# Selection credit that counts other VectorE work, a free step in each recurrence, and attention's second pair moved behind the first `w_pa` job

## The chip, the cores and the metric

The kernel runs on one core of one Trainium2 chip. The metric is the device time of one execution in microseconds, as the median of several runs. Before the change it is 1357.88 us (three runs, 1356.63 to 1357.95).

## The reference

One layer of a hybrid block, batch 1, 512 tokens, width 2048, all in float32:

```python
h = rmsnorm(x, norm_w)
proj = h @ w_in                       # a_q a_f a_i a_g | c_q c_kv k_idx w_idx | b_g | m_a m_b
y_a = hgrn2_branch(a_q, a_f, a_i, a_g, ...)      # gated recurrence, 8 heads of 128, chunks of 64
y_b = dsa_branch(c_q, c_kv, k_idx, w_idx, ...)   # indexer scores -> top 128 keys per query -> attention
merged = sigmoid(m_a) * (y_a @ w_pa) + sigmoid(m_b) * (y_b @ w_pb)
out = rmsnorm(x + merged @ w_out, final_norm_w)
```

Branch A computes, per head, `o = sum over earlier tokens` of decayed key-value products. Branch B scores all visible keys with 16 index heads, keeps the 128 best per query, and runs softmax attention over them with a relative-position bias. Each branch's result is multiplied by a SiLU gate.

## The kernel before, in words

Every large product is made in three float32r passes (`mm3`, L75 to L77): each operand is split into a high and a low part, and high*high, high*low and low*high are accumulated in PSUM. A weight tile is loaded by SyncE (L128), its high part is copied by ScalarE and its low part is subtracted by VectorE (`split`, L71 and L72, tiles `wh` and `wl`).

TensorE is fed by a list of jobs that runs once, in order: projections of x (`feat_job`, `ai_job`), gate products with a seven-product scheme (`pair_job`), the index heads, then the part this change touches, then the two branch projections `w_pa` and `w_pb` and the output product. A `feat_job` with two column tiles does 12 matmuls of 512 columns per weight tile and column tile, evacuates a finished tile, and calls `pump()` (twice as often in the `w_pa` jobs).

`pump()` is what mixes the small work in. There are lanes named hgrn, top, att, norm, misc and t5; each holds Python generators, and one call advances the first generator of each lane to its next `yield`, in that order of lanes. All instructions go to their engine's queue in the order in which they are emitted, and each engine works its queue off in that order. So nothing is decided at run time: where a step stands in the emission sets what it waits behind.

- **hgrn** runs the recurrence of head pairs 3, 2, 0, 1, one generator (`hgrn_gen(p)`) each. It makes levels 1 to 7: at each level TensorE computes small score matmuls (`hl`) from the tile `hqk`, VectorE multiplies `hqk` by the level's decay (L763, 1024 columns) and takes scores into a mask (L769). The scores of a level read the `hqk` that the level before has multiplied. After the levels come transposes of k (`hkt`), copied by ScalarE to `hkd`, state products (`hp`), the states `hst`, outputs (`ho`), a norm by a matmul with ones (`hz`), and the gated result `hy`, split in two and stored to the DRAM tile `ya_d` (L859).
- **top** is the selection (`top_gen`): 3 blocks of queries, 16 rounds each of MAX and MATCH_REPLACE on VectorE (L631, L632) over 256, 384 and 512 columns of the score mask `M`. It works on credit: each call adds 2.7 less `R.load`, each round costs 0.4 + 0.27 per block of 128 columns, and rounds are emitted while credit is positive. `R.load` is set by the hgrn lane to about what its step costs VectorE.
- **att** runs attention for a pair of heads (`att_gen(p)`), and starts once the selection is finished. Its steps: the mask with bias `MB` (GpSimd), scores `lA`, `lB`, `lC` with VectorE adds (L930), exponentials, transposes `tA` to `tC`, values `po`.

The queries, keys and values of head pair p are made by `uqkv(p)`: a job for the queries (`uq_evac`, tiles `aq`) and a job for keys and values (`ukv_job`, tiles `ak`, `av`). All projection results go through one PSUM pool `mmp` of four buffers; a product may start when VectorE and ScalarE have read the buffer's last content.

The order of the jobs from the index on: `ai_job(3)`, `ai_job(2)`, `af_aq(0)`, `af_aq(1)`, `open_att` (which runs all but the last pending recurrence to its end at once), `uqkv(0)`, the gate job of four column tiles (`gate_job(44)`, eight weight tiles; it loads `y_a` back from `ya_d` into the tiles `yh` and `yl`, and after its seventh weight tile `end_hgrn` finishes the last recurrence and loads heads 2 and 3), `uqkv(1)`, and eight `w_pa` jobs with `uqkv(2)` and `uqkv(3)` behind those with j = 4 and j = 8.

Of the kernel before, what the change touches and what calls it, by code (L numbers as in the profile page):

```python
# [43 lines left out]
STILL, MOVED, RANK = 16, 48, 16  # L44
# [6 lines left out]
def hybrid_block(ctx, tc, x, w_in, w_uq, w_qidx, w_ukv, w_pa, w_pb, w_out, rel_bias, final_norm_w,  # L51
# [4 lines left out]
    w_in, w_uq, w_qidx, w_ukv = w_in[0], w_uq[0], w_qidx[0], w_ukv[0]  # L56
# [13 lines left out]
    def split(hi, lo, src):  # L70
        A.activation(hi, src, AF.Copy)  # L71
        V.tensor_tensor(lo, src, hi.bitcast(F32), op=OP.subtract)  # L72
# [22 lines left out]
    yb_d = dram.tile([2, H, 128, T], F32, name="yb_d")  # L95
# [17 lines left out]
    def leave(name):  # L113
        pools.pop(name)[0].__exit__(None, None, None)

    R = SimpleNamespace(load=0.0)


    specs = []
# [16 lines left out]
    def weight_places(at):  # L136
        return [wpool.tile([128, WCAP + 64], FR, name=name)[:, at:at + WCAP] for name in ("wh", "wl")]

    def pair_sums(t, at):


        b = t.rearrange("p (q n) -> p q n", q=4)
        sv = R.g.tile([128, 4, 256], F32, name="sv", bufs=R.sv)
        vh, vl = (a.rearrange("p (q n) -> p q n", q=4) for a in weight_places(at))
        V.tensor_tensor(sv[:, 0:2, :], b[:, 1:3, :], b[:, 0:1, :].to_broadcast([128, 2, 256]), op=OP.add)  # L145
        V.tensor_tensor(sv[:, 2, :], sv[:, 1, :], b[:, 1, :], op=OP.add)
        V.tensor_tensor(sv[:, 3, :], sv[:, 2, :], b[:, 3, :], op=OP.add)
        bh = R.g.tile([128, 3, 256], FR, name="bh", bufs=3)
        bl = R.g.tile([128, 3, 256], FR, name="bl", bufs=3)
        A.activation(bh, b[:, 1:4, :], AF.Copy)  # L150
# [6 lines left out]
    def prep(i, ahead=3):  # L157
        while issued[1] < min(i + ahead, len(specs)):
            j = issued[1]
            if specs[j][3:4] == ("pair",) and not hasattr(R, "g"):  # L160
                if j > i + 1 and lanes["norm"]:
                    break
                open_pairs()
            load_ahead()
            _, kc, n = specs[j][:3]
            t = raws.pop(j)
            if specs[j][3:4] == ("pair",):
                halves[j] = pair_sums(t, 0 if specs[j][4] else R.at)
                issued[1] += 1
                continue  # L170
            if len(specs[j]) > 3 and isinstance(specs[j][3], str):
                both = R.s2.tile([128, 2, WCAP], FR, name="wk", tag=specs[j][3])
                hi, lo = both[:, 0, :], both[:, 1, :]
            else:
                hi, lo = weight_places(*specs[j][3:] or (0,))
            split(hi[:, :kc * n], lo[:, :kc * n], t[:, :kc * n])
            halves[j] = tuple(a[:, :kc * n].rearrange("p (k n) -> p k n", k=kc) for a in (hi, lo))
            issued[1] += 1

# [20 lines left out]
    def drain(name):  # L200
        lane = lanes[name]
        while lane:
            for _ in lane[0]:
                pass
            lane.popleft()

    jobs, hg = [], {}

    def feat_job(src, col, ntile, nk, kc, rhs, evac, before=None, width=T, after=None, place=0,
                 often=False):  # L210
        at = len(specs)
        n = ntile * 128
        for k in range(0, nk, kc):
            specs.append(([(0, n, src[k * 128:(k + kc) * 128, col:col + n])], kc, n, place))

        def run():
            if before:
                before()
            ps = [mmp.tile([128, T], F32, name="acc")[:, 0:width] for _ in range(ntile)]
            for i in range(nk // kc):  # L220
                prep(at + i)
                wh, wl = halves.pop(at + i)
                for c in range(ntile):
                    for k in range(kc):
                        kk = i * kc + k
                        rh, rl = rhs(kk)
                        s = slice(c * 128, c * 128 + 128)
                        mm3(ps[c], wh[:, k, s], wl[:, k, s], rh, rl, kk == 0, kk == nk - 1)
                        if often and k == 1:
                            pump()  # L230
                    if kk == nk - 1:
                        evac(c, ps[c])
                    if ntile < 4 or c % 2:
                        pump()
                if after and i in after:
                    after[i]()

        jobs.append(run)
# [377 lines left out]

    def top_gen():

        credit = 0.0
        V.memset(R.M[:, 0:128], 0.0)  # L620
        for b in range(4):
            V.memset(R.M[0:64, MO[b] + b * 128 + 64:MO[b] + b * 128 + 128], NEG)
        for b in (1, 2, 3):
            m = R.M[:, MO[b]:MO[b] + b * 128 + 128]
            for i in range(16):
                while credit <= 0:
                    yield
                    credit += 2.7 - R.load
                credit -= 0.4 + 0.27 * (b + 1)
                m8 = R.s.tile([128, 8], F32, name="m8", bufs=2)  # L630
                V.max(m8, m)  # L631
                V.match_replace(m, m8, m, GONE)  # L632
                if i == 15:
                    V.tensor_scalar(m, m, -2e38, NEG, op0=OP.is_gt, op1=OP.mult)
# [83 lines left out]
    def aq_evac(p):  # L718
        def evac(c, ps):
            if c == 0:  # L720
                hg[p, "q"] = place(p, [128, 2, T], F32, "hq", "hq")
            q = hg[p, "q"][:, c, :]
            A.activation(q, ps, AF.Sigmoid)
            V.scalar_tensor_tensor(q, ps, 128 ** -0.5, q, op0=OP.mult, op1=OP.mult)
            if c == 1:
                lanes["hgrn"].append(hgrn_gen(p))
        return evac

    def hgrn_gen(p):
# [11 lines left out]
        q, k = qk[:, 0], qk[:, 1]  # L741
        qf, kf = (a.rearrange("p c t -> p (c t)") for a in (q, k))
        yield
        for _ in range({2: 1, 0: 2, 1: 2}.get(p, 0)):
            yield

        def scores(l, ps):
# [24 lines left out]
        for l in range(1, 8):  # L772
            R.load = (0, 2.9, 2.2, 2.0, 1.9, 1.8, 1.5, 1.4)[l]
            if l == 4:
                G.memset(S, 0.0)
            if l == 1:
                first = bank("hl")
                scores(0, first)
            ps = bank("hl")
            scores(l, ps)  # L780
            tot = decay(l)
            if l == 1:
                take(0, first)
            if l < 6:
                take(l, ps)
            else:
                m = 1 << (l - 1)
                for h in range(0, 128, 2 * m):
                    A.activation(S[h:h + m, :, h + m:h + 2 * m],
                                 ps[h:h + m, 0:8 * m].rearrange("p (n t) -> p n t", n=8), AF.Copy)  # L790
            if l == 6:
                for h in range(0, 128, 32):
                    A.activation(S[h:h + 32, :, h:h + 32], near[h:h + 32], AF.Copy)
            yield

        R.load = 0.0
        kd = R.h.tile([128, 2, 3, 128], F32, name="hkd")
# [57 lines left out]
        for c in range(2):  # L855
            y = [place(p, [128, T], FR, f"hy{i}", (("hkd", "hst"), ("hq", "hS"))[i][c]) for i in range(2)]
            split(*y, sq[:, c])
            for i in range(2):
                late[1].append(lambda y=y[i], i=i, h=2 * p + c: SP.dma_start(ya_d[i, h], y.bitcast(F32)))  # L859
        yield  # L860


    at_ = {}

    def uq_evac(p):
        def evac(c, ps):
            if c == 0:
                at_[p, "q"] = [R.a.tile([128, 2, T], FR, name=f"aq{i}") for i in range(2)]
            hi, lo = (a[:, c, :] for a in at_[p, "q"])
            A.activation(hi, ps, AF.Copy, scale=128 ** -0.5)  # L870
            V.scalar_tensor_tensor(lo, ps, 128 ** -0.5, hi.bitcast(F32), op0=OP.mult, op1=OP.subtract)
        return evac
# [150 lines left out]
    def open_pairs():  # L1023
        drain("norm")
        drain("misc")
        flush()
        flush()
        leave("norms")
        R.g = enter("pairs")
        R.g.tile([128, STILL], F32, name="gap")  # L1030
        R.sv, R.at = 2, STILL
# [105 lines left out]
    c_rhs = lambda k: (R.cqh[:, k, :], R.cql[:, k, :])  # L1137
# [56 lines left out]
        feat_job(w_in, p * 256, 2, NK, 4, x_rhs, aq_evac(p))  # L1194

    def uqkv(p):
        feat_job(w_uq, p * 256, 2, 4, 4, c_rhs, uq_evac(p), place=RANK)
        ukv_job(p)

    jobs.append(end_index)  # L1200
# [10 lines left out]
    def load_y(y, src, h0, h1):  # L1211
        for h in range(h0, h1, 2):
            for i in range(2):
                SP.dma_start(y[i][h // 4][:, h % 4:h % 4 + 2, :].bitcast(F32),
                             src[i, h:h + 2].rearrange("h p t -> p h t"))
# [20 lines left out]

    def y_rhs(name):
        return lambda k: tuple(y[k // 4][:, k % 4, :] for y in getattr(R, name))

    uqkv(1)  # L1240
    jobs.append(lambda: load_y(R.yb, yb_d, 0, 2))

    mh, ml, mg = [], [], {}

# [76 lines left out]
    for j in range(0, NK, 2):  # L1321
        if j + 2 < NK:
            jobs.append(lambda j=j: load_gates(16, j + 2))
        feat_job(w_pa, j * 128, 2, H, 4, y_rhs("ya"), pa_evac(j), often=True)
        if j in (4, 8):
            uqkv(j // 4 + 1)
        if j in (6, 10):
            jobs.append(lambda h=j // 2 - 1: load_y(R.yb, yb_d, h, h + 2))
    jobs.append(open_merge)
# [230 lines left out]
```

## Time and profile before

| | |
|---|---|
| median of 3 runs | 1357.88 us |
| profiled execution, its own time | 1356.24 us |
| its span, first to last instruction | 1354.4 us |
| TensorE busy | 1339.9 us (99%) |
| VectorE busy | 1070.7 us (79%) |
| ScalarE busy | 656.1 us (48%) |
| GpSimd busy | 41.3 us (3%) |
| DMA | 205.82 MB, mean 152 GB/s |
| mean granted TensorE clock | 0.997 |

The time outside the span is 1356.24 - 1354.4 = 1.8 us. A busy TensorE is not TensorE at its peak: ends of matmuls are modelled, and a matmul that waits a little shows as a longer distance between two starts. In the timelines below a row is a start, a duration, and in brackets the idle time before it with what ended it. The stretch from 690 us (end of the index) to 960 us (start of the `w_pa` jobs) is where the recurrences, the selection and attention's first pair run.

### The profile page before, as it was taken

How to read it: one execution, taken by the hardware profiler on the slowest of the kernel's cores; microseconds unless marked ns; L12 is line 12 of the kernel's file. 1: busy time of each engine (PE TensorE's matmuls, PEld its weight loads, DVE VectorE, ACT ScalarE, POOL GpSimd, SP SyncE). 2: the span in 40 equal slices, each digit the busy share in tenths (PEclk: the TensorE clock that was granted, in tenths of full speed). 3: DMA queues.
4: the chain of work that ended last, by engine and by line, in shares of the span. 5: the costliest groups of instructions: out<-in, count | busy, mean ns of one | idle time of the engine just before them, and what ended most of it. 6: DMA issues, size and time to landing. Idle time of an engine off the chain costs nothing.

```text
span 1354.4 us, 26556 instructions
## 1 busy us (share of the span) xinstructions
PE 1339.9 (99%) x10884; PEld 1242.7 (92%) x10884; DVE 1070.7 (79%) x1705; ACT 656.1 (48%) x1039; POOL 41.3 (3%) x54
## 2 busy tenths in 40 slices
PE   9999999999999999999999999999999999999997
PEld 9988999999999999999999787788888888899996
DVE  7777889998898888886789889585556658899856
ACT  6455554455544444444764454635443433454434
POOL 3000000000000000000000000020101100000000
PEclk9999999999999999999999999999999999999999
DMA  6343445543445444445324523244855556643454
GB/s 240 94 124 109 141 143 157 160 146 111 127 141 156 140 141 140 141 143 169 126 77 127 171 78 127 81 161 145 291 176 197 180 186 210 210 157 115 158 208 173
DMA packets 141290, 205.82 MB, mean 152 GB/s; under 512 B 8672, under 2 KB 82032, under 8 KB 141040
## 3 DMA queue, kind: packets, MB, share of 16 engines
q1 hardware_dynamic: 140592, 203.78, 47.1%
q8 instruction: 85, 1.39, 0.4%
q10 hardware_dynamic: 576, 0.35, 0.1%
q14 instruction: 37, 0.30, 0.1%
HBM read 168.42 MB, written 35.68 MB: 151 GB/s over the span
## 4 chain that ended last, share of the span: by engine, by line
PE 90%; DVE 5%; ACT 2%; DMA 1%; issue 1%; SPq 0%; ACTq 0%
PE pp L75 15%; PE pp L77 15%; PE pp L76 15%; PE acc L75 12%; PE acc L77 12%; PE acc L76 12%; PE hl L80 1%; PE ho L80 1%; DMA wr<-in_w_in_dram 1%; DVE wl L72 1%; PE sc L75 1%; PE sc L76 1%; PE sc L77 1%; DVE hqk L763 1%; DVE M L632 1%
## 5 line engine op out<-in xcount | busy, mean ns | idle before, releaser
L150 ACT ACTIVATE bh<-wr 128x768 fp32r<-128x768 f32 x128 | 108.2, 845 | 216.9 <-issue 108.8
L152 ACT ACTIVATE wh<-sv 128x512 fp32r<-128x512 f32 x256 | 152.2, 623 | 85.3 <-DVE sv L145 68.1
L75 PE MATMUL pp<-sh,wh 128*128 128x256 f32 x624 | 172.8, 277 | 0.0
L77 PE MATMUL pp<-sh,wl 128*128 128x256 f32 x624 | 172.8, 277 | 0.0
L76 PE MATMUL pp<-sl,wh 128*128 128x256 f32 x624 | 172.7, 277 | 0.0
L72 DVE TENSOR_TENSOR wl<-wr,wh 128x1024 fp32r<-128x1024 f32 (+1 forms) x104 | 125.3, 1204 | 56.8 <-ACT wh L71 56.5
L154 DVE TENSOR_TENSOR wl<-sv,wh 128x1024 fp32r<-128x1024 f32 x128 | 156.4, 1222 | 6.1
L153 DVE TENSOR_TENSOR bl<-wr,bh 128x768 fp32r<-128x768 f32 x128 | 122.2, 955 | 48.4 <-ACT bh L150 47.8
L71 ACT ACTIVATE wh<-wr 128x1024 fp32r<-128x1024 f32 (+1 forms) x104 | 108.0, 1040 | 104.8 <-PE acc L76 54.5
L75 PE MATMUL acc<-xh,wh 128*128 128x512 f32 x304 | 121.7, 400 | 0.0
L77 PE MATMUL acc<-xh,wl 128*128 128x512 f32 x304 | 118.8, 391 | 0.0
L76 PE MATMUL acc<-xl,wh 128*128 128x512 f32 x304 | 118.5, 390 | 0.0
L75 PEld LDWEIGHTS pp<-sh,wh 128*128 128x128 f32 x624 | 117.3, 188 | 0.0
L76 PEld LDWEIGHTS pp<-sl,wh 128*128 128x128 f32 x624 | 117.3, 188 | 0.0
L77 PEld LDWEIGHTS pp<-sh,wl 128*128 128x128 f32 x624 | 117.3, 188 | 0.0
L75 PE MATMUL pp<-xh,bh 128*128 128x256 f32 x416 | 114.9, 276 | 0.0
L77 PE MATMUL pp<-xh,bl 128*128 128x256 f32 x416 | 114.9, 276 | 0.0
L76 PE MATMUL pp<-xl,bh 128*128 128x256 f32 x416 | 114.9, 276 | 0.0
L75 PE MATMUL acc<-yh,wh 128*128 128x512 f32 x256 | 100.2, 391 | 0.0
L77 PE MATMUL acc<-yh,wl 128*128 128x512 f32 x256 | 99.8, 390 | 0.0
L76 PE MATMUL acc<-yl,wh 128*128 128x512 f32 x256 | 99.7, 390 | 0.0
L145 DVE TENSOR_TENSOR sv<-wr 128x512 f32<-128x512 f32 x128 | 87.8, 686 | 8.2 <-DMA wr<-in_w_out_dram 4.1
(385 smaller groups left out, 3618.5 us busy)
## 6 DMA issues: line engine op xcount, KB each, us to landing
wr<-in_w_in_dram SPq DMA_DIRECT2D x136, 512.0 KB, 3.6
wr<-in_w_out_dram SPq DMA_DIRECT2D x32, 512.0 KB, 3.8
mg<-gate_d SPq DMA_DIRECT2D x48, 256.0 KB, 4.4
gate_d<-c SPq DMA_DIRECT2D x44, 256.0 KB, 5.0
wr<-in_w_in_dram SPq DMA_DIRECT2D x36, 256.0 KB, 2.9
wr<-in_w_pa_dram SPq DMA_DIRECT2D x16, 512.0 KB, 4.3
wr<-in_w_pb_dram SPq DMA_DIRECT2D x16, 512.0 KB, 4.2
wr<-in_w_qidx_dram SPq DMA_DIRECT2D x8, 512.0 KB, 3.4
```

The lines of the kernel that those rows point to most:

```text
L71: A.activation(hi, src, AF.Copy)
L72: V.tensor_tensor(lo, src, hi.bitcast(F32), op=OP.subtract)
L75: PE.matmul(ps, lh, rh, start=first, stop=False, skip_group_check=True)
L76: PE.matmul(ps, lh, rl, start=False, stop=False, skip_group_check=True)
L77: PE.matmul(ps, ll, rh, start=False, stop=last, skip_group_check=True)
L80: PE.matmul(ps, l, r, start=first, stop=last, skip_group_check=True)
L145: V.tensor_tensor(sv[:, 0:2, :], b[:, 1:3, :], b[:, 0:1, :].to_broadcast([128, 2, 256]), op=OP.add)
L150: A.activation(bh, b[:, 1:4, :], AF.Copy)
L152: A.activation(vh[:, i:i + 2, :], sv[:, i:i + 2, :], AF.Copy)
L153: V.tensor_tensor(bl, b[:, 1:4, :], bh.bitcast(F32), op=OP.subtract)
L154: V.tensor_tensor(vl, sv, vh.bitcast(F32), op=OP.subtract)
L632: V.match_replace(m, m8, m, GONE)
```

## The change

It has five pieces.

1. The selection's credit: each call adds 2.95 (was 2.7) less `R.load`, and less `R.extra`, which is 1.2 for each weight tile split (L72) and 0.7 for each recurrence query tile (L724) emitted since the last call.
2. In `hgrn_gen`, one call passes between level 1 and level 2 in which the generator does nothing and `R.load` is 0. The idle calls ahead of level 1 go from 2 to 1 for pairs 0 and 1, and stay 1 for pair 2 and 0 for pair 3.
3. `R.load` is set to 0 in those idle calls and at the end.
4. `uqkv(1)` moves from behind the gate job to behind the first `w_pa` job, and the load of branch B's heads 0 and 1 with it.
5. Before the query job of pair 1 the lanes top and att are drained.

```diff
-    R = SimpleNamespace(load=0.0)
+    R = SimpleNamespace(load=0.0, extra=0.0)
...
             split(hi[:, :kc * n], lo[:, :kc * n], t[:, :kc * n])
+            R.extra += 1.2
...
-        credit = 0.0
+        credit = R.extra = 0.0
...
                 while credit <= 0:
+                    R.extra = 0.0
                     yield
-                    credit += 2.7 - R.load
+                    credit += 2.95 - R.load - R.extra
...
             V.scalar_tensor_tensor(q, ps, 128 ** -0.5, q, op0=OP.mult, op1=OP.mult)
+            R.extra += 0.7
...
         yield
-        for _ in range({2: 1, 0: 2, 1: 2}.get(p, 0)):
+        R.load = 0.0
+        for _ in range({2: 1, 0: 1, 1: 1}.get(p, 0)):
             yield
...
             yield
+            if l == 1:
+                R.load = 0.0
+                yield
...
         yield
+        R.load = 0.0
...
-        feat_job(w_uq, p * 256, 2, 4, 4, c_rhs, uq_evac(p), place=RANK)
+        feat_job(w_uq, p * 256, 2, 4, 4, c_rhs, uq_evac(p), place=RANK,
+                 before=lambda: p == 1 and (drain("top"), drain("att")))
         ukv_job(p)
...
-    uqkv(1)
-    jobs.append(lambda: load_y(R.yb, yb_d, 0, 2))
...
         feat_job(w_pa, j * 128, 2, H, 4, y_rhs("ya"), pa_evac(j), often=True)
-        if j in (4, 8):
+        if j in (0, 4, 8):
             uqkv(j // 4 + 1)
+        if j == 0:
+            jobs.append(lambda: load_y(R.yb, yb_d, 0, 2))
```

Three places show how instructions move. Each row is the kernel's line, the operation, output and inputs, and the output's shape; the changed file's lines are up to eight higher (its L742 and L767 are L739 and L763 before, its L879 is L871, its L1223 is L1214).

**VectorE in `uqkv(0)`.** `aq` is the low part of a query tile, `ak` and `av` those of keys and values, `wl` of a weight tile; `hqk` and `hnear` belong to the recurrence of pair 1; MAX and MATCH_REPLACE with `m` and `M` are selection rounds. Before:

```order
L871 SCALAR_TENSOR_TENSOR aq_10563<-acc,aq_10562 128x512
L739 TENSOR_TENSOR hqk<-hq,hf 128x1024
L871 SCALAR_TENSOR_TENSOR aq_10563<-acc,aq_10562 128x512
L72 TENSOR_TENSOR wl<-wr,wh 128x1024
L72 TENSOR_TENSOR ak_10595<-acc,ak_10594 128x512 x2
L72 TENSOR_TENSOR av_10597<-acc,av_10596 128x512 x2
L763 TENSOR_TENSOR hqk<-hqk,hf 128x2x512
L765 TENSOR_TENSOR tot_10715<-hf 128x512
L769 COPY_PREDICATED hnear<-levels,hl 128x256 x2
L72 TENSOR_TENSOR wl<-wr,wh 128x1024
L763 TENSOR_TENSOR hqk<-hqk,tot_10715 128x2x256x2
```

In the change, up to the first level's decay:

```order
L879 SCALAR_TENSOR_TENSOR aq_10547<-acc,aq_10546 128x512
L742 TENSOR_TENSOR hqk<-hq,hf 128x1024
L633 MAX m_10560<-M 128x8
L634 MATCH_REPLACE M<-m_10560,M 128x512
L879 SCALAR_TENSOR_TENSOR aq_10547<-acc,aq_10546 128x512
L633 MAX m_10577<-M 128x8
L634 MATCH_REPLACE M<-m_10577,M 128x512
L633 MAX m_10580<-M 128x8
L634 MATCH_REPLACE M<-m_10580,M 128x512
L72 TENSOR_TENSOR wl<-wr,wh 128x1024
L72 TENSOR_TENSOR ak_10588<-acc,ak_10587 128x512 x2
L767 TENSOR_TENSOR hqk<-hqk,hf 128x2x512
```

and behind it, up to the second level's decay:

```order
L769 TENSOR_TENSOR tot_10678<-hf 128x512
L773 COPY_PREDICATED hnear<-levels,hl 128x256 x2
L72 TENSOR_TENSOR av_10590<-acc,av_10589 128x512 x2
L633 MAX m_10712<-M 128x8
L634 MATCH_REPLACE M<-m_10712,M 128x512
L72 TENSOR_TENSOR wl<-wr,wh 128x1024
L767 TENSOR_TENSOR hqk<-hqk,tot_10678 128x2x256x2
```

Four selection rounds of 512 columns, which stood before `open_att`, now stand inside this job, three of them ahead of `ak`; and the first level's decay stands ahead of `av`, since its scores now come before the value products on TensorE.

**TensorE in `open_att`.** The recurrence of pair 0 runs to its end here, with no projection matmuls between its stages. Before, the state products `hp` have projection matmuls on both sides, and the last of these are followed by `ho` and `hz`:

```order
L80 MATMUL hp<-hv,hkd 128x128 [waits Activation_49]
L80 MATMUL hp<-hv,hkd 128x128 x2
L75 MATMUL acc<-xh_91,wh 128x512
L76 MATMUL acc<-xl_94,wh 128x512
L77 MATMUL acc<-xh_91,wl 128x512
```

In the change the same stage has none:

```order
L808 MATMUL hkt<-ident,hqk 128x128 [waits PE_49]
L808 MATMUL hkt<-ident,hqk 128x128 x2
L80 MATMUL hp<-hv,hkd 128x128 [waits Activation_49]
L80 MATMUL hp<-hv,hkd 128x128 x2
L80 MATMUL ho<-hS,hv 128x128 [waits PE_49,Pool_49]
L80 MATMUL ho<-hS,hv 128x128
L80 MATMUL ho<-hqk,hst 128x128 [waits Activation_49]
```

The transposes and the state products have moved into the stretch without cover.

**TensorE at the end of the gate job.** Before, the query job of pair 1 follows (here behind the last value matmul `po` of head 1):

```order
L77 MATMUL po<-PT,av_10597 128x128
L75 MATMUL acc<-cqh,wh 128x512 [waits Activation_49]
L76 MATMUL acc<-cql,wh 128x512
L77 MATMUL acc<-cqh,wl 128x512
L75 MATMUL acc<-cqh,wh 128x512
```

In the change the first `w_pa` job follows; `DMAHW` names the semaphore of a load:

```order
L77 MATMUL acc<-xh_91,wl 128x512
L75 MATMUL acc<-yh,wh 128x512 [waits DMAHW7_49,Activation_49]
L76 MATMUL acc<-yl,wh 128x512 [waits DMAHW0_49]
L77 MATMUL acc<-yh,wl 128x512 [waits DVE_49]
L75 MATMUL acc<-yh,wh 128x512
L76 MATMUL acc<-yl,wh 128x512
L77 MATMUL acc<-yh,wl 128x512
L75 MATMUL acc<-yh,wh 128x512 [waits DMAHW2_49]
L76 MATMUL acc<-yl,wh 128x512 [waits DMAHW3_49]
L77 MATMUL acc<-yh,wl 128x512
```

The seventh matmul of that job is the first to read head 2 of `y_a`, and waits for the load of heads 2 and 3, which is issued at the end of the gate job's seventh weight tile; the 60 matmuls of `uqkv(1)` no longer stand between.

## The prediction

> **What bounds the kernel.** I read the page's head, then the waits of TensorE, then stretches of the timeline around the places where the change moves work.
>
> ```profile
> span 1354.4 us, 26556 instructions
> PE 1339.9 (99%) x10884; PEld 1242.7 (92%) x10884; DVE 1070.7 (79%) x1705; ACT 656.1 (48%) x1039; POOL 41.3 (3%) x54
> ```
>
> TensorE is the bound, and the change adds or removes no work on it. So only its waits can move. The table of waits for the whole run holds, in the stretch that is touched:
>
> ```profile
> PE hl L80 <- DVE hqk L763: 1.6, 3, 0.7
> PE hl L80 <- issue: 0.9, 1, 0.9
> PE hz L80 <- ACT hzh L71: 0.7, 2, 0.4
> PE hz L80 <- DVE hzl L72: 0.5, 2, 0.3
> ```
>
> ```profile
> 715.39 0.70 PE L80 MATMUL hl<-hqk 128*32 128x32 f32 x32 [0.70 <-DVE hqk L763]
> 766.04 0.45 PE L80 MATMUL hl<-hqk 128*32 128x32 f32 x31 [0.57 <-DVE hqk L763]
> 832.89 0.52 PE L80 MATMUL hl<-hqk 128*32 128x32 f32 x36 [0.35 <-DVE hqk L763]
> ```
>
> Three waits for a decay on VectorE (1.6 us), one of 0.9 us in which nothing shows what was awaited, and four for the norm in `open_att`. That is all a better order could win: 3.7 us. The `open_att` waits have a tail, seen in the windows (columns: busy time of PE, PEld, DVE, ACT, POOL, then granted clock, DMA share, GB/s):
>
> ```profile
> 866.00:868.00 2.00, 1.27 (x3) 0.56 (x3) 0.93 (x2) 1.95 (x5) 0.00 (x0) 1.00 0.00 0
> 868.00:870.00 2.00, 1.71 (x5) 1.19 (x5) 0.46 (x1) 1.99 (x3) 0.00 (x0) 0.74 0.00 0
> 870.00:872.00 2.00, 2.00 (x6) 1.59 (x5) 0.00 (x0) 1.97 (x3) 0.00 (x0) 0.50 0.00 0
> 872.00:874.00 2.00, 2.00 (x9) 1.61 (x9) 1.30 (x2) 0.63 (x1) 0.00 (x0) 0.91 0.00 0
> ```
>
> After some 2 us of broken idle the clock was granted at half: 2 x (0.26 + 0.50 + 0.09) = 1.7 us lost. A wait of a few us costs its own length and up to 1.7 us more.
>
> **Part 1: the free step.** The waits at 766.04 and 832.89 are second-level scores waiting for the first level's decay. With a call between them TensorE brings another 2.8 us of projection matmuls (below), so both go: -0.57 - 0.35 = -0.9 us. The wait at 715.39 is the sixth level of the first recurrence, where norm work of VectorE is queued ahead of the decay; the free step delays all levels, the selection starts a call earlier, and the same norm work stands in the same place. I take 0, bounds -0.7 and +0.5 (half a decay of 1.22 us).
>
> **Part 2: `uqkv(0)`.** The credit now charges weight splits, so the selection is slower and its last rounds fall into this job, which has no charge for its own `aq`, `ak` and `av`. Its VectorE queue and two TensorE marks before:
>
> ```profile
> 878.32 0.69 DVE L871 SCALAR_TENSOR_TENSOR aq<-acc,aq 128x512 fp32r<-128x512 f32 x1
> 878.92 1.21 DVE L739 TENSOR_TENSOR hqk<-hq,hf 128x1024 f32<-128x1024 f32 x1
> 880.06 0.68 DVE L871 SCALAR_TENSOR_TENSOR aq<-acc,aq 128x512 fp32r<-128x512 f32 x1
> 880.66 1.21 DVE L72 TENSOR_TENSOR wl<-wr,wh 128x1024 fp32r<-128x1024 f32 x1
> 881.79 1.28 DVE L72 TENSOR_TENSOR ak<-acc,ak 128x512 fp32r<-128x512 f32 x2
> 882.99 1.28 DVE L72 TENSOR_TENSOR av<-acc,av 128x512 fp32r<-128x512 f32 x2
> 884.18 1.22 DVE L763 TENSOR_TENSOR hqk<-hqk,hf 128x1024 f32<-128x1024 f32 x1
> ```
>
> ```profile
> 878.43 0.39 PE L77 MATMUL acc<-ckh,wl 128*128 128x512 f32 x1
> 879.06 0.38 PE L75 MATMUL acc<-wh,ckh 128*128 128x256 f32 x1 [0.25 <-DVE aq L871]
> 882.41 0.73 PE L80 MATMUL hl<-hq,hqk 128*32 128x32 f32 x62
> 883.67 0.50 PE L75 MATMUL acc<-xh,wh 128*128 128x512 f32 x1
> ```
>
> ```profile
> L631 DVE MAX8 m<-M 128x8 f32<-128x512 f32 x16 | 11.0, 687 | 0.1
> L632 DVE MATCH_REPLACE8 M<-m,M 128x512 f32<-128x512 f32 x16 | 10.8, 676 | 0.0
> ```
>
> VectorE is without a gap here, and starts each instruction about 0.08 us before the last one ends. A selection round is 0.69 + 0.68 = 1.4 us. I walk the new order in the old clock. VectorE: first `aq` to 879.0, `hqk` to 880.1, one round to 881.5, second `aq` to 882.1, two rounds to 884.8, `wl` to 886.0, `ak` at 886.6 and 887.2, first decay to 888.4, its two helpers (some 1.4), `av` at 890.4 and 891.0, a round to 892.3, `wl` to 893.4, second decay to 894.6.
>
> TensorE: the key products end at 878.66. The scores follow at once now; their first half is free, the second needs `hqk` at 880.1: a wait of 1.1, then on to 880.7. Value products take 1.4 each (879.06 to 882.41 less one short wait): to 882.1 and, after the second `aq`, to 883.6. The gate job's first tile needs the third PSUM buffer of four, which `ak` frees at 886.6: a wait of 3.0. Two tiles of 1.4 and the second-level scores bring it to 890.4, when `av` is just done, and two more tiles to 893.1, where the third level waits for the second decay until 894.6: 1.5. Together 1.1 + 3.0 + 1.5 = 5.6, against about 0.7 of small waits there before: **+4.9 us**. What is late next is weight tiles; they are split two tiles ahead, over 10 us, and hold. Bounds: 3.0, the middle wait alone, and 6.5 if the clock halves in addition (at half clock the tiles run 2.8 longer, but 1.5 of that lies in the third wait).
>
> **Part 3: `open_att`.** The free step makes the recurrence of pair 0 a step later, so `hkt` and `hp` fall into the drained stretch. `hp` needs ScalarE's copies of `hkt`, which now stand behind the query tile's sigmoid. The three costs, the first row from the chain of waits, the others from ScalarE's timeline:
>
> ```profile
> 855.22 0.65 PE hkt L801 x6
> ```
>
> ```profile
> 855.58 0.87 ACT L802 ACTIVATE hkd<-hkt 128x384 f32<-128x384 f32 x2 [2.69 <-PE hkt L801]
> 858.64 0.60 ACT L723 ACTIVATE hq<-acc 128x512 f32<-128x512 f32 x1 [1.24 <-PE acc L77]
> ```
>
> Sigmoid 0.60, one copy 0.87 / 2, an estimated 0.25 for two hand-overs like the one at 879.06, less 0.65 in which the transposes run: 0.60 + 0.44 + 0.25 - 0.65 = **+0.65 us** of idle. The later stages wait as before. Bounds 0.4 and 1.0 (the second copy too).
>
> **Part 4: the first `w_pa` job comes early.** `uqkv(1)` stood between the last recurrence and the reader of its result. Where it began and where `w_pa` began:
>
> ```profile
> 949.45 0.45 PE L75 MATMUL acc<-cqh,wh 128*128 128x512 f32 x1
> 960.58 0.40 PE L75 MATMUL acc<-yh,wh 128*128 128x512 f32 x1
> ```
>
> 11.13 us, for 48 matmuls of 512 columns and their like in smaller pieces: 0.232 us each. On the other side stands the way of `y_a` heads 2 and 3 through DRAM. First VectorE, then SyncE's queue, then the DMA view (count, KB each, median us from issue to landing):
>
> ```profile
> 925.05 0.42 DVE L930 CUSTOM_DVE_ANT_0 P<-lA,M 128x256 f32<-128x256 f32 x1
> ...
> 927.45 0.17 DVE L941 TENSOR_SCALAR mx<-mx 128x4 f32<-128x4 f32 x1
> ```
>
> ```profile
> 941.13 0.75 DVE L851 SCALAR_TENSOR_TENSOR hqk<-ho,cols,hqk 128x512 f32<-128x512 f32 x1
> ...
> 945.44 1.28 DVE L72 TENSOR_TENSOR hy<-hqk,hy 128x512 fp32r<-128x512 f32 x2
> ```
>
> ```profile
> 949.53 0.37 SPq L1214 DMA_DIRECT2D yl<-ya_d  x1
> ```
>
> ```profile
> ya_d<-hy SPq DMA_DIRECT2D x3, 256.0 KB, 2.4
> yl<-ya_d SPq DMA_DIRECT2D x1, 512.0 KB, 4.8
> ```
>
> The last `hy` ended at 946.72, the load of `yl` was issued at 949.53 (it waits for the stores' landing) and landed at 954.35: 7.6 us from `hy` to data. The reader, the seventh matmul of `w_pa`, came at 960.58 + 1.4, so 7.6 us were spare. Taking out 11.1 turns that into a lack of 3.5 with nothing else moved. What moved besides is VectorE's order near the end. I count from Z, the moment TensorE begins the value products `po` in the changed gate job. TensorE behind Z: `po` 1.74, the next scores 1.74 (7.5 matmuls' worth each), 36 gate matmuls 8.35, six of `w_pa` 1.39: it asks for head 2 at Z + 13.2. VectorE behind Z: `po` ends at 1.74, `ag`, ScalarE's split and `ay` at some 4.0 (0.69 + 0.63 + 0.69 and the hand-overs), attention's adds to 6.6 (925.05 to 927.62), the four gate products to 9.5 (941.13 to 943.99), `hy` to 10.8. Plus 7.6 is Z + 18.4. The lack is 5.2; the sixth matmul's wait for `yl` heads 0 and 1 is none, those are long there. I take **+4.9 us**, since `ay` may start a little before `po` is fully done; bounds 3.5 (the shift alone) and 5.7. Queued behind on SyncE's ring, the `mg` and weight loads wait too, but weights are two tiles ahead.
>
> Afterwards comes the clock. At `open_att` broken idle of 2 us was followed by half clock for 3.4 us (868.96 to 872.37), a loss of 1.7. A full stop of 4.9 us should cost the same: **+1.7 us**, bounds 0 and 3.4.
>
> [...]
>
> **Behind that** the jobs' order is one that the old kernel had, only with pair numbers shifted, and I cost it at 0: attention's `MB` on GpSimd is emitted two calls ahead of its reader, and VectorE had slack there. Without this cover it would be a wait for `MB` of a few us at the first `w_pa` calls, in which TensorE stands anyway.
>
> **The sum.** -0.9 + 0 + 4.9 + 0.65 + 4.9 + 1.7 = +11.25. Of the 0.9 us "issue" wait no cause shows; moved code may lose it or not, so half, -0.45. Together +10.8. The profiled execution's own time is 1356.24 us (span 1354.4 and 1.8 around it), giving 1367.0; the median of the runs is 1357.88, 1.6 higher, giving 1368.7. I take the middle, 1367.8 us. With the bounds of the parts (3.0 to 6.5, 3.5 to 5.7, 0 to 3.4, 0.4 to 1.0, and -1.6 to -0.4 for what is won) the change lies between +5.3 and +16.2; not all ends come at once, so the forecast's own range is 1363 to 1372.
>
> **The rivals.**
>
> *Only one of the two stalls.* In `uqkv(0)` my walk has VectorE about 3 us late for `ak`. Had VectorE entered the job 3 us less loaded, since the slower selection left it idle earlier, only the waits at the ends remain. For it: calls with many weight splits get fewer rounds, which shortens the queue ahead of the job. Against: 878.32 to 885.4 has no gap. Then 10.8 - 4.0 = +6.8; where instead the stall at `w_pa` has only its lower bound and no clock loss, it is 10.8 - 1.4 - 1.7 = +7.7. About 1364.5.
>
> *Faster.* The waits for decays and the "issue" wait go (-2.5 with the one at 715.39), and VectorE has so much slack before `uqkv(0)` that the selection's rounds end ahead of `ak`, and the recurrence of pair 1 ends 5 us sooner against TensorE, as the lightened VectorE would allow, so that the load is back in time. It decides once both lacks, 3.0 and 4.9, are covered. For it: VectorE's 79% leave slack on average. Against: the free step delays the last recurrence, and the 7.6 us of the round trip are no work of VectorE. -2.5 gives 1355.
>
> *No effect of weight.* Rounds emitted late or early hit no wait, and `w_pa`'s stall is about made up by what is won: within 2.7 us, some 1358. Against: part 4 with the shift alone is already +3.5.
>
> **Chances.** A measurement of this kernel can tell about 0.2% (2.7 us). Forecast 0.71, one stall 0.16, no effect 0.06, faster 0.07. So slower 0.87, same 0.06, faster 0.07. The range for 8 in 10 takes in most of the one-stall case below and the clock's upper bounds above: 1361 to 1372.
>
> **What would show it.** Right: TensorE's first wait in `uqkv(0)`'s successor job for `ak` on VectorE, some 3 us, followed by `hl` waiting for `hqk` at the third level; no second-level waits like those at 766.04 and 832.89; one wait of 4 to 5 us of a `w_pa` matmul for the load of `yh` or `yl`, and half clock in the windows behind it. Wrong: no wait for a DMA at `w_pa` (part 4 falls), or VectorE with gaps before `ak` (part 2 falls), or new waits for `MB` or weight tiles behind `w_pa`, which I cost at nothing.

## The result, and the profile after

The changed kernel takes 1369.42 us (median of 5 runs, 1369.11 to 1370.27), the kernel before beside it 1356.63 us (5 runs): a ratio of 1.0093, with a 95% interval of 1.0079 to 1.0108. It is 12.8 us slower; the forecast was 10.8 us slower, at 1367.8. The profiled execution has 1369.11 us of its own time and a span of 1367.3 us, 12.9 more than before.

The page's head shows no more work on TensorE, only more waiting: its busy time grows by only 1.9 us, the span by 12.9.

```profile
span 1367.3 us, 26572 instructions
PE 1341.8 (98%) x10884; PEld 1243.0 (91%) x10884; DVE 1072.1 (78%) x1705; ACT 659.1 (48%) x1041; POOL 36.6 (3%) x54
```

TensorE's waits between 715 and 990 us (total, times, longest):

```profile
PE acc L75 <- DVE ak L72: 2.7, 1, 2.7
PE acc L76 <- DMA yl<-ya_d: 2.7, 1, 2.7
PE acc L75 <- DMA yh<-ya_d: 2.1, 1, 2.1
PE hl L80 <- DVE hqk L767: 1.8, 2, 1.2
PE acc L75 <- ACT gs L1135: 1.5, 1, 1.5
PE hl L80 <- ACT hqk L741: 1.4, 1, 1.4
PE hl L80 <- DVE hqk L742: 0.9, 1, 0.9
```

The wait without a releaser (0.9 us) is gone, and so are the second-level waits. Two groups are new. The first is `uqkv(0)`, on TensorE's timeline:

```profile
877.19 0.76 PE L80 MATMUL hl<-hq,hqk 128*32 128x32 f32 x64 [1.40 <-ACT hqk L741]
878.86 0.75 PE L80 MATMUL hl<-hqk 128*32 128x32 f32 x64 [0.90 <-DVE hqk L742]
...
885.40 0.50 PE L75 MATMUL acc<-xh,wh 128*128 128x512 f32 x1 [2.73 <-DVE ak L72]
...
893.40 0.76 PE L80 MATMUL hl<-hqk 128*32 128x32 f32 x64 [1.24 <-DVE hqk L767]
```

`ak`, on VectorE, stands behind three selection rounds and a weight split, as walked, and starts at 884.66:

```profile
883.53 1.22 DVE L72 TENSOR_TENSOR wl<-wr,wh 128x1024 fp32r<-128x1024 f32 x1
884.66 1.28 DVE L72 TENSOR_TENSOR ak<-acc,ak 128x512 fp32r<-128x512 f32 x2
```

The second group is the first `w_pa` job:

```profile
949.88 0.39 PE L77 MATMUL acc<-xh,wl 128*128 128x512 f32 x1
951.74 0.50 PE L75 MATMUL acc<-yh,wh 128*128 128x512 f32 x1 [1.48 <-ACT gs L1135]
...
953.00 0.40 PE L77 MATMUL acc<-yh,wl 128*128 128x512 f32 x1
955.50 0.79 PE L75 MATMUL acc<-yh,wh 128*128 128x512 f32 x1 [2.11 <-DMA yh<-ya_d]
958.95 0.79 PE L76 MATMUL acc<-yl,wh 128*128 128x512 f32 x1 [2.65 <-DMA yl<-ya_d]
```

Taken by the distance of the starts, less the usual 0.23, the three stops cost 951.74 - 949.88 - 0.23 = 1.63, then 2.27 and 3.22: 7.1 us. The bracketed waits show less (6.2): they begin at the modelled end of the matmul ahead, which is 0.39 or 0.40 us behind its start, where starts are 0.23 apart. Behind them, the clock (windows; the last three columns are granted clock, DMA share and GB/s):

```profile
956.00:958.00 2.00, 0.30 (x1) 0.00 (x0) 1.27 (x4) 1.99 (x3) 0.00 (x0) 0.50 0.67 195
958.00:960.00 2.00, 1.05 (x3) 0.86 (x4) 0.85 (x1) 1.12 (x2) 0.00 (x0) 0.50 1.03 394
```

From 958.95 to about 962.3 matmuls ran at half clock: 1.6 us lost by the distance of their starts.

### The profile page after: what moved, and what is told of

Its sections match the earlier page's. It is cut to its first block, busy times and chain, and to the rows that moved or that the text cites. A ratio compares the mean times of both kernels' runs of the same rounds, so it can differ in the third digit from the quotient of the medians.

```text
span 1367.3 us, 26572 instructions
## 1 busy us (share of the span) xinstructions
PE 1341.8 (98%) x10884; PEld 1243.0 (91%) x10884; DVE 1072.1 (78%) x1705; ACT 659.1 (48%) x1041; POOL 36.6 (3%) x54
## 4 chain that ended last, share of the span: by engine, by line
PE 91%; DVE 5%; ACT 2%; DMA 2%; issue 1%; SPq 0%; DVEq 0%; ACTq 0%
PE pp L77 15%; PE pp L76 15%; PE pp L75 15%; PE acc L75 13%; PE acc L77 13%; PE acc L76 13%; PE hl L80 1%; DMA xt<-in_x_t_dram 1%; PE ho L80 1%; DVE hqk L767 1%; PE sc L75 1%; PE sc L76 1%; PE sc L77 1%; DMA yl<-ya_d 0%; PE hp L80 0%
## 5 line engine op out<-in xcount | busy, mean ns | idle before, releaser
L72 DVE TENSOR_TENSOR wl<-wr,wh 128x1024 fp32r<-128x1024 f32 (+1 forms) x104 | 125.8, 1210 | 58.1 <-ACT wh L71 57.7
```

## The experiments

The experiments undo one piece of the change, or two together, or try what a piece is worth alone. Times are medians; the ratio to the kernel before, in the runs of the same chip, is given beside them.

### Pair 1 back at its old place

```diff
+    uqkv(1)
+    jobs.append(lambda: load_y(R.yb, yb_d, 0, 2))
     mh, ml, mg = [], [], {}
...
-        if j in (0, 4, 8):
+        if j in (4, 8):
             uqkv(j // 4 + 1)
```

(and the two lines that drain the lanes and load branch B's heads behind the first `w_pa` job are gone.)

> The changed kernel with its fourth and fifth piece undone: the query, key and value jobs of pair 1 stand behind the gate job again; credit and free step stay. Theory (a third of the loss is the selection's rounds in uqkv(0), the larger part the first w_pa job that comes before its data): the waits for ScalarE's gs (1.5 us), for yh (2.1) and yl (2.7) and the half clock behind them vanish, so about 8.5 us less than the changed kernel's 1369.4, that is 1361; the waits in uqkv(0) (1.4 + 0.9 + 2.7 + 1.2) stay. Rival (the load was not late by itself, only because VectorE fell behind in uqkv(0)): the delay is handed on to pair 1's queries and the time stays above 1366.

Measured: 1368.2 us, ratio 1.0076 (1.0059 to 1.0093). The theory said 1361 and missed; the rival's number was right, and its reason in part: the delay is handed on, but to attention's values and not to pair 1's queries. The waits for `yh` and `yl` did vanish. In their place stand waits of attention's values (same stretch as above):

```profile
PE acc L75 <- DVE ak L72: 2.7, 1, 2.7
PE po L75 <- ACT PT L71: 2.0, 1, 2.0
PE acc L75 <- ACT gs L1135: 1.5, 1, 1.5
PE po L76 <- DVE P L72: 1.1, 1, 1.1
```

The selection with the new credit ends later, so attention's second head still runs when pair 1's queries are made (the first scores `lA` come at 910.9 on TensorE, at 891.0 in the kernel before). ScalarE then has, in a row, the gate tiles, the exponentials and the table loads between them (its timeline):

```profile
953.46 1.28 ACT L954 ACT_TABLE_LOAD   x1
...
957.07 1.28 ACT L1135 ACT_TABLE_LOAD   x1
...
961.23 0.62 ACT L71 ACTIVATE PT<-tA 128x512 fp32r<-128x512 f32 x1
```

`PT` comes at 961.23, and `po` waits for it and then for VectorE's `P`. This execution had half clock in three places (868.0 to 871.4, 885.0 to 891.9, and from 963.5 to at least 965.9), the changed kernel only in one, but that is not what makes it long: another execution of the same kernel, with a mean granted clock of 0.998 instead of 0.994, took 1368.40 us. So the stop at `w_pa` is one way in which the change's cost shows, and not the whole of it: with the late selection, the old place of pair 1 is nearly as dear as the new one.

### The old credit

```diff
-                    credit += 2.95 - R.load - R.extra
+                    credit += 2.7 - R.load
```

> The changed kernel with the old credit (2.7 less the recurrence's load, nothing for weight splits or query tiles); everything else stays. No selection round stands in uqkv(0) any more. Theory: the wait for ak (2.7 us) and the third-level wait (1.2 to 1.4) go, the two at the head of pair 1's first level (1.4 and 0.9) stay, since they come from the shorter run-up of the recurrence and not from the credit; the stop at w_pa stays within 1 us. About 4.3 us less: 1365. Rival (a slower VectorE there also makes y_a late, so both losses have one cause): the stop at w_pa shrinks with it by 3 us or more, and the time is below 1361.

Measured: 1363.81 us, ratio 1.0043 (1.0028 to 1.0058), 5.6 less than the changed kernel (expected 4.3).

```profile
PE acc L75 <- DMA yh<-ya_d: 2.1, 1, 2.1
PE acc L76 <- DMA yl<-ya_d: 1.9, 1, 1.9
PE hl L80 <- ACT hqk L741: 1.4, 1, 1.4
PE hl L80 <- DVE hqk L742: 0.9, 1, 0.9
```

The wait for `ak` is gone and the two at the head of the recurrence stay, as the theory said. The stop at `w_pa` loses the wait for ScalarE's `gs` but keeps `yh` and `yl`: 4.0 in place of 6.2. It shrinks by 2.2, more than the 1 us of the theory and less than the 3 of the rival, so the credit has a part in the stop too.

### The last recurrence ended one weight tile earlier

```diff
-                  6: end_hgrn, 7:
+                  5: end_hgrn, 7:
```

> The changed kernel with the end of the last recurrence, and the load of heads 2 and 3 with it, one weight tile earlier in the gate job (behind its sixth instead of its seventh). On VectorE the four gate products and hy then stand ahead of attention's ag, ay and adds. Theory: hy ends about 4.5 us earlier, the load lands 4.5 us earlier, and of the waits for yh and yl (4.8 us) under 1 us is left, and no half clock behind it: 4 to 6 us less than the changed kernel, 1364. Rival (what makes the load late is the DMA queues at the w_pa job, not when hy is done): the load is issued earlier but lands within 1.5 us of where it did, and the time stays above 1367.5. A second rival: attention's adds come later and TensorE waits for its exponentials instead.

Measured: 1361.58 us, ratio 1.0031 (1.0019 to 1.0043), 7.8 less than the changed kernel. No wait for `yh` or `yl` is left. VectorE's `hy` and SyncE's load, first here, then in the changed kernel:

```profile
941.15 1.47 DVE L72 TENSOR_TENSOR hy<-hqk,hy 128x512 fp32r<-128x512 f32 x2
945.31 0.37 SPq L1223 DMA_DIRECT2D yl<-ya_d  x1
```

```profile
948.08 1.47 DVE L72 TENSOR_TENSOR hy<-hqk,hy 128x512 fp32r<-128x512 f32 x2
952.45 0.37 SPq L1223 DMA_DIRECT2D yl<-ya_d  x1
```

They come 6.9 and 7.1 us earlier (0.4 of it is a lead that this execution already has at the first `po`, 937.70 for 938.09), where 4.5 was expected: not only attention's adds (2.57) but also `ag`, `ay` and the weight split now stand behind `hy`, and in the changed kernel the gate products stood behind VectorE's waits for them. The second rival is there, but small: TensorE waits 1.1 us for VectorE's `P` at the transposes `tA`. In `uqkv(0)`, whose instructions are the same, the wait for `ak` shows 1.3 instead of 2.7, because the matmuls ahead of it ran at half clock (878.6 to 882.1) and filled the time: from the last `hz` of `open_att` to the end of that wait it is 18.31 us in both kernels.

### Both undone, pair 1 still late

The two edits above together (old credit, `5: end_hgrn`).

> The changed kernel with the old credit and with the last recurrence ended one weight tile earlier: both main losses undone, pair 1 still behind the first w_pa job. If the two losses are separate, their gains add: 1369.4 - 5.6 - 7.8 = 1356.0. If they share a piece (the wait for yh and yl had already shrunk a little with the old credit, from 5.5 to 4.4, and each of them had another half clock), 1358. If the late place of pair 1 costs something by itself, 1360 or more.

Measured: 1356.99 us, ratio 1.0001 (0.9992 to 1.0010): as the kernel before. The gains add, but for 1 us (5.6 + 7.8 = 13.4 against 12.4). In 715 to 990 us these waits of TensorE are left, none of them for `y_a` or `ak`:

```profile
PE hl L80 <- DVE hqk L742: 0.8, 1, 0.8
PE hl L80 <- DVE hqk L767: 0.7, 1, 0.7
PE hz L80 <- ACT hzh L71: 0.7, 2, 0.4
...
PE hp L80 <- ACT hkd L809: 0.4, 1, 0.4
```

So the place of pair 1 costs nothing once `y_a` is back in time; what costs is that `w_pa` asks before.

### The free step alone

The kernel before with the second and third piece only.

> The kernel before with the second and third piece alone (free step, shorter run-up for pairs 0 and 1, load set to 0); old credit, pair 1 at its old place. Theory: the second-level waits (0.6 and 0.4 us) go, the two waits at the head of pair 1's first level (2.3) come, the copies in open_att cost 0.4; half clock at open_att may or may not fall into place (1.7). So 1356.6 - 1.0 + 2.3 + 0.4 = 1358.3, between 1356 and 1359. Rival (the free step frees VectorE over the whole stretch): 1354 or less.

Measured: 1357.97 us, ratio 1.0005 (0.9995 to 1.0014): no difference that can be told, as the theory's 1358.3 had it. The second-level waits are gone, 1.4 and 0.9 at pair 1's first level and 0.4 in `open_att` are there.

This kernel differs from "Pair 1 back at its old place" in the credit alone, and from "The old credit" in the place of pair 1 alone, with its drain. The four times together (us):

| | pair 1 at its old place | pair 1 behind the first `w_pa` job |
|---|---|---|
| old credit | 1357.97 | 1363.81 |
| new credit | 1368.20 | 1369.42 |

The credit costs 10.2 at the old place and 5.6 at the new one, the place 5.8 with the old credit and 1.2 with the new one. The two do not add, and the credit is the dearer of them.

### The free step with the old run-up for pair 1

```diff
-        for _ in range({2: 1, 0: 1, 1: 1}.get(p, 0)):
+        for _ in range({2: 1, 0: 1, 1: 2}.get(p, 0)):
```

in the kernel with the free step alone.

> The kernel with the free step alone, with pair 1's run-up back at two calls, so that its first level's scores come behind the value products as in the kernel before. Theory (the two waits of 2.3 us at the first level, and the half clock that followed in 880 to 883, are the price of the shorter run-up): they vanish, and what is left against the kernel before is the won second-level and issue waits (-2.0 with those of pairs 2 and 0), the copies in open_att (+0.4) and a wait of 0.35 at the level handed out with the selection. 1355.3, faster than before by about 0.1%. Rival (a recurrence that ends a call later makes y_a late even with pair 1 ahead of w_pa): a wait of 1 us or more for yl, and 1357.5 or more.

Measured: 1358.39 us, ratio 1.0014 (1.0005 to 1.0023). The expected gain did not come. The two waits at the first level are gone, and with them the half clock of 880.5 to 883.9; half clock follows `open_att` (868.7 to 872.1), as in the kernel before. The second-level and "issue" waits are gone too, but new ones stand elsewhere: 0.20 and 0.46 in the first recurrence (703.84 and 711.10), 0.22 at 905.69, 0.74 for `gs`, and 0.4 in `open_att`. The rival's number fits, but its wait for `yl` is not there.

### The changed kernel with the old run-up for pair 1

The same edit in the changed kernel.

> The changed kernel with pair 1's run-up back at two calls. Theory: the waits of 1.4 and 0.9 at the first level go, and those for ak (2.7) and at the third level (1.2) fall to half, since the first decay stands behind av again; but the recurrence ends a call later against TensorE, so the wait for yh and yl grows by up to 2.8. Together within 2 us of 1369.4. Rival (run-up is the cause of the loss in uqkv(0), the end is set by the drain behind the seventh weight tile and so does not move): 1365.5 or less.

Measured: 1365.10 us, ratio 1.0064 (1.0050 to 1.0078), 4.3 less than the changed kernel: the rival's number, but not its reason.

```profile
PE acc L76 <- DMA yl<-ya_d: 3.6, 1, 3.6
PE acc L75 <- DVE aq L879: 3.2, 2, 1.8
PE acc L75 <- DVE ak L72: 1.7, 1, 1.7
...
PE acc L75 <- ACT gs L1135: 0.6, 1, 0.6
...
PE acc L75 <- DMA yh<-ya_d: 0.3, 1, 0.3
```

In `uqkv(0)` two waits for `aq` (1.81 and 1.43) stand in place of those at the head, and the gate job's first matmul, which waits for `ak`, starts 18.31 us behind the last `hz` of `open_att`, as in the changed kernel. VectorE's queue sets that moment, wherever TensorE waits ahead of it. The gain lies behind it: the third level waits 0.46 instead of 1.24, and attention is further on (first `lA` at 895.7, 909.6 in the changed kernel), so that a head's transposes are done before the gate job ends and its values `po` run inside the stop at `w_pa` (from 951.68). From the gate job's last matmul to the first that reads the awaited `yl` it is 9.07 us in both kernels. The last recurrence is finished at `end_hgrn` in either case, and a call more at its head did not make `hy` later. The profiled execution took 1366.50 us, the longest of four, so its trace shows only 2.6 of the gain.

### The gate loads behind `w_pa`'s first weight tile

```diff
-    jobs.append(lambda: load_gates(16, 0))
...
-        if j + 2 < NK:
+        if j and j + 2 < NK:
...
-        feat_job(w_pa, j * 128, 2, H, 4, y_rhs("ya"), pa_evac(j), often=True)
+        feat_job(w_pa, j * 128, 2, H, 4, y_rhs("ya"), pa_evac(j), often=True,
+                 after=None if j else {0: lambda: (load_gates(16, 0), load_gates(16, 2))})
```

> The changed kernel with the four loads of gate tiles mg (256 KB each) issued behind the first weight tile of the first w_pa job instead of ahead of that job; nothing else moves. In the changed kernel the load of yl took 6.5 us from issue to use, where the row of before had 4.8. Theory (these loads and the weight load share the DMA engines with yl): yl lands 1.5 to 2 us earlier and the time falls to 1367.5, the waits for yh and for gs staying. Rival (the landing is set by the stores of y_a ahead of it): the waits stay as they are, 1369.4. Third: the gate tiles come too late for the evacuation, and VectorE's wait is passed on to TensorE.

Measured: 1368.69 us, ratio 1.0089 (1.0075 to 1.0103): no gain. The DMA view between 948 and 956 us of this kernel:

```profile
yl<-ya_d SPq DMA_DIRECT2D x1, 512.0 KB, 6.6
```

`yl` still takes 6.6 us, without the gate loads. Why it takes longer here than the 4.8 us before stays open. The weight load, the stores of `gs` and `yh` itself were issued close to it, but so they were in the kernel before. Over the profiles of these runs the same load takes between 4.7 us (the last recurrence ended one weight tile earlier) and 7.1 us (the changed kernel with the old run-up).

### The free step for pair 2 alone

```diff
             yield
-            if l == 1:
+            if l == 1 and p == 2:
                 R.load = 0.0
                 yield
```

in the kernel with the free step alone, with the old run-ups.

> The kernel before with the free step in the recurrence of pair 2 alone (and the load set to 0 in idle calls); run-ups, credit and pair 1 as before. In every kernel with the free step so far the second-level wait of pair 2 (0.57 us) and the wait with no releaser behind it (0.9) are gone. Theory: these 1.5 us are what the free step is worth, and the costs (0.4 in open_att, 2.3 in pair 1's first level) belong to pairs 0 and 1 alone: 1356.7 - 1.5 = 1355.2, a ratio of 0.9989, at the edge of what can be told. Rival (the moved selection rounds bring new waits of the same size): 1356.7.

Measured: 1358.26 us, ratio 1.0007 (0.9998 to 1.0015). New waits came, as the rival said. The second-level wait of pair 2 is gone, but one of 1.55 us stands at its third level, and that at pair 0's second level is 1.02 (0.35 before):

```profile
773.31 0.76 PE L80 MATMUL hl<-hqk 128*32 128x32 f32 x64 [1.55 <-DVE hqk L767]
```

VectorE's timeline ahead of it shows why: a free call with no load earns the selection 2.7 of credit, two rounds of 384 columns are emitted, and they stand ahead of the decay.

```profile
769.66 0.55 DVE L633 MAX8 m<-M 128x8 f32<-128x384 f32 x1
...
772.04 1.22 DVE L767 TENSOR_TENSOR hqk<-hqk,tot 128x1024 f32<-128x1024 f32 x1
```

### Two variants on top of it

The first shortens pair 0's run-up (`{2: 1, 0: 1, 1: 2}`), the second puts pair 1 behind the first `w_pa` job and `end_hgrn` behind the sixth weight tile.

> The kernel with the free step for pair 2 alone and, besides, pair 0's run-up at one call instead of two, so that its recurrence reaches open_att one call further. Theory: one stage more is covered by projection matmuls there; the waits for hzh and hzl (1.2 by the table of waits, 2.2 by the distance of the matmuls) stand three stages later and stay, the wait at the second level of pair 0 (0.4) may move to its first: within 0.7 us of the kernel with the step alone. Rival (the broken idle in open_att gets shorter and the half clock behind it does not come): 2 us less.

Measured: 1360.98 us, ratio 1.0035 (1.0021 to 1.0048), slower: pair 0's second level waits 1.92 us for its decay, which stands behind three selection rounds of 512 columns and a weight split, and then 1.21 more with no releaser, and half clock follows (835.1 to 842.0). The profiled execution took 1363.33 us, 2.4 above the median, so the typical one may have less half clock than its trace.

> The kernel with the free step for pair 2 alone, with pair 1 behind the first w_pa job and the last recurrence ended behind the sixth weight tile of the gate job. Theory (pair 1's place costs nothing once y_a is back in time): the same as the kernel with the step alone, 1355.2. Rival (it costs the cover of the last steps): waits at the end of the recurrence or for yl, 1357 or more.

Measured: 1357.97 us, ratio 1.0012 (1.0003 to 1.0020), the same as the kernel with pair 2's step (1358.26), though both missed the 1355.2 of the theory: the late place of pair 1 is free here too, and no wait for `yh` or `yl` is in its trace. No variant beat the kernel before.

## Why the prediction was right, point by point

The direction, the two places and most of the size held: +12.8 against +10.8. By the terms of the sum, with TensorE's losses taken by the distance of starts:

| term | predicted | measured in the profile |
|---|---|---|
| second-level waits, pairs 2 and 0 | -0.9 | -0.9, both gone |
| sixth-level wait of the first recurrence | 0 | +0.1 (0.77 in place of 0.70) |
| "issue" wait | -0.45 | -0.9, gone |
| `open_att`, state products uncovered | +0.65 | +0.4, the wait of `hp` for `hkd` |
| half clock behind `open_att` | left in place | not there in this execution, but nothing gained: it is part of the next row |
| `uqkv(0)`, from the last `hz` of `open_att` | +4.9 | 15.15 to 18.31 at the gate job's first matmul, +3.2, and +1.3 at the third level: +4.5 |
| first `w_pa` job | +4.9 | +7.1 |
| half clock behind it | +1.7 | +1.6 |

These measured terms sum to 11.9 of the span's 12.9. A level wait near 908.6 (0.70 by its start's distance, where 0.27 stood before) makes 0.4 of the rest.

**Part 2, `uqkv(0)`.** The walk gave the waits 1.1, 3.0 and 1.5; they came as 0.90, 2.73 and 1.24, and the whole as 4.5 for 4.9. The first scores also waited 1.40 for ScalarE's `hqk` (L741), where the walk has "their first half is free". The walk had taken the old clock, with half clock behind `open_att`; at full clock TensorE came 1.7 us earlier and waited. In the two runs that had the half clock (pair 1 back, both undone) the wait for L741 is not there, as walked. The credit is the cause of the lateness of `ak`: with the old credit the gate job's first matmul starts 15.42 us behind the last `hz` (both undone), or 16.75 and 16.93 where half clock fell among the value products (the old credit, the free step alone), 15.15 before the change (and 15.14 with the free step and the old run-up). The run-up is not: with the new credit the old run-up leaves 18.31 and only changes which matmuls wait. The two waits at its head cost time only with the old credit, where `ak` is not late.

**Part 3.** The mechanism was right, 0.4 in place of 0.65: one bracketed wait of `hp`.

**Part 4, `w_pa`.** Z, the first `po`, was at 938.09, and TensorE would have asked for head 2 at 938.09 + 13.2 = 951.3. `hy` ended at 949.55, Z + 11.5, where Z + 10.8 was forecast. The one wait of 4 to 5 us came as three stops, 7.1 us together. The mis-sized term is the round trip: from `hy` to data 949.55 to 958.95, 9.4 us, where 7.6 was taken from the trace of before; its load of `yl` alone went from 4.8 to 6.5 us:

```profile
yl<-ya_d SPq DMA_DIRECT2D x1, 512.0 KB, 6.5
```

The forecast also left ScalarE's table load ahead of `gs` unnamed (1.28 us from 949.80); it shows as the first 1.48 of the stop. It probably hides in the load's lateness, since the data would have been awaited anyway, but no run takes it away alone.

**The clock.** The loss of 1.7 behind the stop was right. The 1.7 us "lost" behind `open_att` were misread. The granted clock there was 1.00 in the changed kernel, although the waits are the same, and yet the gate job starts as far behind the last `hz` as in the run with pair 1 back, which had the half clock. First the changed kernel's last `hz` (its 885.40 is shown above, 18.31 later), then the two marks with pair 1 back, again 18.31 apart:

```profile
867.09 0.50 PE L80 MATMUL hz<-hzl,ones_r 128*128 128x512 f32 x1 [0.28 <-DVE hzl L72]
```

```profile
867.53 0.50 PE L80 MATMUL hz<-hzl,ones_r 128*128 128x512 f32 x1 [0.28 <-DVE hzl L72]
885.84 0.80 PE L75 MATMUL acc<-xh,wh 128*128 128x512 f32 x1 [2.73 <-DVE ak L72]
```

In the order of the kernel before it is the same. There the value products start at 879.06, 10.54 us behind the last `hz`, with half clock and a wait of 0.25 for `aq`. With the free step for pair 2 alone, at full clock, it is 10.55, with a wait of 1.83:

```profile
868.52 0.50 PE L80 MATMUL hz<-hzl,ones_r 128*128 128x512 f32 x1 [0.29 <-DVE hzl L72]
```

```profile
869.34 0.50 PE L80 MATMUL hz<-hzl,ones_r 128*128 128x512 f32 x1 [0.28 <-DVE hzl L72]
879.89 0.39 PE L75 MATMUL acc<-wh,ckh 128*128 128x256 f32 x1 [1.83 <-DVE aq L879]
```

VectorE delivers `aq` or `ak` when it does, and a slower TensorE only waits less for it. Behind the stop at `w_pa` no such wait follows, so there the 1.6 us are lost. The forecast, which left the first half clock in place and added only the second, came out right on both, on the first by luck: it took those 1.7 us for a loss.

**The rivals.** "Only one of the two stalls" did not occur. "Faster" rested on VectorE's slack: the run that ended the recurrence earlier shows that the lack at `w_pa` could indeed be covered, but by an edit, not by the credit. What the credit did instead was to move four rounds behind `open_att` and to delay attention (first `lA` at 909.6, 891.0 before), which the run with pair 1 at its old place showed as waits of `po`. The forecast did not have that cost at all; with pair 1 late it stayed hidden.

## What to carry to other kernels

When a consumer is moved ahead, list what its old place gave time to: here 11 us of projection matmuls hid a trip through DRAM whose spare was 7.6. A wait removed by a free call can come back if a background lane is paid in calls: with the step for pair 2 alone two rounds filled the queue ahead of the next decay, and a wait of 1.55 us stood at the next level. And two losses found in one trace are only known to be separate when each has been undone alone and both together; undoing the piece that seemed to cost most gave back 1.2 us of the 8.7 that its place in the trace shows, and 5.8 once the credit was the old one. A short wait or a stretch of half clock ahead of a wait that another engine ends was no cost by itself here (18.31 us from the last `hz` to the gate job's first matmul, with half clock and without): measure from an event ahead of both to the start behind the last wait.

## What the runs showed of the hardware

The granted clock did not follow the length of a stop. The four waits for `hz` in `open_att` lie within 3 us and are the same in all 13 profiles (two for `hzh`, 0.7 us, and two for `hzl`, 0.5; the longest distance lost is 0.68 us in the changed kernel); half clock followed in the kernel before, with pair 1 back, with the free step and the old run-up, and with both undone, and did not follow in the other nine. A single stop of 2.73 us for `ak` was followed by full clock in the changed kernel (1.00 in the windows from 884 to 894) and by half clock with pair 1 back:

```profile
884.00:886.00 2.00, 0.16 (x1) 0.17 (x1) 2.00 (x4) 0.69 (x1) 0.00 (x0) 0.76 0.01 4
886.00:888.00 2.00, 2.00 (x5) 1.61 (x6) 2.00 (x3) 0.00 (x0) 0.00 (x0) 0.50 0.84 228
```

The half-clock stretches of which the windows show both ends had two lengths: about 3.4 us in nine cases (868.96 to 872.37 in the kernel before) and about 6.8 in three (885.04 to 891.87 here, 955.48 to 962.31 in the changed kernel). Two executions show two such stretches each: they start 17.07 us apart here (867.97 and 885.04) and 51.20 us apart with pair 0's run-up shortened (835.13 and 886.33), 5.0 and 15.0 times 3.41.

In the changed kernel half clock began at 955.48, behind stops of 1.48 and 2.11 us, each shorter than the 2.73 that full clock followed.

Nor did TensorE's busy time ahead of it decide by itself. In the 3.41 us ahead of a half-clock stretch TensorE was busy for 2.22 us in the kernel before (865.55 to 868.96) and for 1.48 with pair 1 back (ahead of 885.04); in the changed kernel it was busy for 0.68 us from 881.99 to 885.40, and full clock followed. What decides it stays open.
